# One tile instead of two for seven token sums, and the end of the output projection in a written order

## The chip, the core and the metric

The kernel runs on one core of a Trainium2 chip. The metric is the device time of one execution in microseconds (us), and the number compared is the median of the runs. A profiled execution leaves a trace with the start and duration of every instruction on the engines: TensorE (PE, and PEld for its weight loads), VectorE (DVE), ScalarE (ACT), GpSimd (POOL) and SyncE (SP, which issues the transfers).

## What is computed

Two residual blocks run over 256 latent tokens and 256 context tokens with 1024 features each. A block is a feed-forward network (FFN), a mixer, and a second FFN; the mixer is a short convolution in block 0 and grouped attention in block 1. In block 1 the context ends after the attention's keys and values. Ahead of each of the three parts stands the same normalization, and it is what the change is about:

```python
def _rms(t, g):
    t32 = t.astype(jnp.float32)
    y = t32 * lax.rsqrt(jnp.mean(t32 * t32, axis=-1, keepdims=True) + NORM_EPS)
    return y.astype(t.dtype) * g

def _modulate(t, g, shift, scale):
    return _rms(t, g) * (1 + scale) + shift

def _swiglu(h, w13, w2):
    gte, up = jnp.split(h @ w13, 2, axis=-1)
    return (jax.nn.silu(gte) * up) @ w2
```

So for every token the squares of its 1024 features are summed (a token sum), and the features are divided by the root of their mean.

## The kernel before, in words

The activations `x` lie transposed: 128 features on the partitions, eight row tiles (`KT`, counted by k or m), and 512 columns, the two streams s = 0 (latents) and s = 1 (context) of 256 tokens each. Matrix products are kept near float32 by splitting each operand into a rounded high part and a low part and adding three products (`mm3`, L146 to L148). ScalarE makes the high parts (L122 `wh<-wr` for weights) and VectorE the low parts (L123 and L526 `wl<-wr,wh`, L496 `bl<-hr,mod,bh` for activations).

**How a token sum is made.** While a projection writes new row tiles of `x`, ScalarE squares each tile and VectorE adds the squares into one tile `acc`. Seven of the eight squares are added this way; the last stays in a tile of its own. The sum over the 128 partitions is then made on TensorE: `sums_of` (L264) multiplies each 128-token piece, as stationary operand, with a column of ones, and for each of the two pieces it accumulates over two tiles, `acc` and the last square. That is four matmuls for one stream, and a float32 matmul leaves two records in the trace. ScalarE takes the root (L272 `rs<-ss`), VectorE the reciprocal (L279 `ri<-rs`), and `rms_rows` (L284 `ss<-cst,ri`) spreads it over the partitions on TensorE again.

**Borders.** Four of the five later norms lie in a border: `open_border` writes, for both streams, the last two row tiles of the old part's projection and the beginning of the next part in one order by hand, which holds for TensorE, VectorE, ScalarE and SyncE. There `late` is the matmuls of a row tile, `fin` (L452) adds the gated result into `x`, `square` (L460) squares it, `add` (L465) adds the first of the two squares into `acc`, `sums`, `root`, `inv` and `rows` make the norm, `mult` (L481) applies it, and `hi` (L488) and `lo` (L496) make the parts that the next matmuls read; `whi` and `wlo` (L521, L526) split the next weights; `share` puts in units of other work for VectorE (L165). The border after a projection with 8 tiles (the convolution's) is `short`, the others have 11. The borders are (block, part): (0,1), (0,2), (1,0) and (1,1). The four calls of `sums(0)` and the four of `sums(1)` are eight token sums. `sums(1)` stands in the next part, behind 16 matmuls that need stream 0 alone (L545), and behind it come 8 that read the first four low parts of stream 0.

**The ninth sum** is that of the last FFN (1,2). Its norm is taken out of the matmuls: the FFN's first products (`first_mm`) read the scaled `x` (`xa`) before the norm is known, and the root is applied to the products. It follows the attention's output projection, whose loop over m the scheduler orders; then a block in written order begins. The token sum stands between the fourth and the fifth row tile of the first FFN product.

**The start.** The very first norm has its own code (L1159), for which `fill` (L1080) puts 17 matmuls on a constant tile ahead of everything, with the spreading of a vector (L1272) behind them.

## Time and profile before

| what | value |
|---|---|
| median of 3 runs | 1550.32 us (1549.9 to 1550.5) |
| the profiled execution | 1550.0 us, span 1548.2 us |
| granted TensorE clock | 1.000 |
| busy: PE, PEld, DVE, ACT, POOL | 1543.1, 1417.7, 1309.1, 763.4, 28.9 us |
| records of the nine later token sums (L264) | 72 of 10286 |

The span is the time from the program's first instruction to its last; the execution's own time is 1.8 us longer. In a row of the timeline stand start, duration, engine, line, operation, output and inputs, shapes and a count, and in brackets the idle time of that engine ahead of it with what ended it. Records of one engine overlap a little, so that the next start can lie ahead of an end.

### The profile page before, as it was taken

The numbers are of one execution on the slowest core, as the hardware profiler recorded it, in microseconds if no ns is written. First come the engines' busy times: TensorE is split into PE (matmuls) and PEld (weight loads), VectorE is DVE, ScalarE is ACT, GpSimd is POOL, SyncE is SP. The second block draws the span as 40 slices with busy tenths as digits, with TensorE's granted clock in tenths as the row PEclk, the third lists the DMA queues.
The fourth block names the chain that finished last, engine by engine and source line by source line (L and its number), as shares of the span: only waits on it lengthen the run. The fifth ranks groups of instructions, "written<-read, shape, count | busy, mean of one in ns | idle before, by whom it ended". The sixth has DMA issues, their size and how long they took to land.

```text
span 1548.2 us, 25395 instructions
## 1 busy us (share of the span) xinstructions
PE 1543.1 (100%) x10286; PEld 1417.7 (92%) x10286; DVE 1309.1 (85%) x1946; ACT 763.4 (49%) x1286; POOL 28.9 (2%) x24
## 2 busy tenths in 40 slices
PE   9999999999999999999999999999999999999999
PEld 7899899989888899988999899988999899998888
DVE  6988889987999689987998989987998777888653
ACT  5554255536222475532554475522554365776551
POOL 0000000000000000000000000000000002220000
PEclk9999999999999999999999999999999999999999
DMA  9333633354565323355333633356444743256551
GB/s 358 136 112 131 209 124 121 125 195 171 183 215 201 136 92 114 114 183 193 123 128 125 224 111 109 115 185 232 137 134 172 260 153 120 97 185 244 189 175 71
DMA packets 52005, 247.72 MB, mean 160 GB/s; under 512 B 6064, under 2 KB 9264, under 8 KB 36656
## 3 DMA queue, kind: packets, MB, share of 16 engines
q1 hardware_dynamic: 51600, 245.91, 46.3%
q8 instruction: 80, 1.31, 0.4%
q14 instruction: 37, 0.30, 0.1%
q10 hardware_dynamic: 288, 0.19, 0.0%
HBM read 243.72 MB, written 1.05 MB: 158 GB/s over the span
## 4 chain that ended last, share of the span: by engine, by line
PE 99%; DMA 0%; ACT 0%; DVE 0%; issue 0%; DVEq 0%; ACTq 0%
PE py L146 9%; PE py L147 9%; PE py L148 9%; PE p L146 7%; PE p L148 7%; PE p L147 7%; PE q L148 5%; PE q L146 5%; PE q L147 5%; PE py L1997 3%; PE pu L1997 3%; PE pg L1997 3%; PE pg L1318 1%; PE pv L146 1%; PE pv L148 1%; PE pg L545 1%
## 5 line engine op out<-in xcount | busy, mean ns | idle before, releaser
L165 DVE CUSTOM_DVE_ANT_0 junk<-wm,scbc,cst 128x1024 bf16<-128x1024 f32 x224 | 286.8, 1281 | 32.1 <-DMA wm<-in_modT 30.5
L122 ACT ACTIVATE wh<-wr 128x1024 fp32r<-128x1024 f32 (+1 forms) x196 | 177.6, 925 | 213.5 <-PE py L147 130.4
L123 DVE TENSOR_TENSOR wl<-wr,wh 128x1024 fp32r<-128x1024 f32 (+1 forms) x196 | 205.4, 1059 | 52.2 <-PE py L1997 22.9
L146 PE MATMUL py<-gh,wh 128*128 128x512 f32 (+1 forms) x594 | 217.8, 367 | 0.0
L147 PE MATMUL py<-gl,wh 128*128 128x512 f32 (+1 forms) x594 | 217.3, 366 | 0.0
L148 PE MATMUL py<-gh,wl 128*128 128x512 f32 (+1 forms) x594 | 217.1, 365 | 0.0
L773 ACT ACTIVATE wh<-wr 128x1024 fp32r<-128x1024 f32 x165 | 169.5, 1056 | 85.6 <-DVE wr L796 67.4
L776 DVE TENSOR_TENSOR wl<-wr,wh 128x1024 fp32r<-128x1024 f32 x165 | 196.7, 1217 | 15.3 <-ACT wh L773 15.3
L148 PEld LDWEIGHTS py<-gh,wl 128*128 128x128 f32 x594 | 112.0, 189 | 18.0
L146 PEld LDWEIGHTS py<-gh,wh 128*128 128x128 f32 x594 | 112.1, 189 | 17.7
L147 PEld LDWEIGHTS py<-gl,wh 128*128 128x128 f32 x594 | 112.1, 189 | 17.2
L148 PE MATMUL p<-th,wl 128*128 128x256 f32 x440 | 124.5, 283 | 0.0
L147 PE MATMUL p<-tl,wh 128*128 128x256 f32 x440 | 124.5, 283 | 0.0
L146 PE MATMUL p<-th,wh 128*128 128x256 f32 x440 | 124.5, 283 | 0.0
L146 PE MATMUL q<-bh,wh 128*128 128x256 f32 x304 | 86.0, 283 | 0.0
L147 PE MATMUL q<-bl,wh 128*128 128x256 f32 x304 | 86.0, 283 | 0.0
L148 PE MATMUL q<-bh,wl 128*128 128x256 f32 x304 | 86.0, 283 | 0.0
L146 PEld LDWEIGHTS p<-th,wh 128*128 128x128 f32 x440 | 84.5, 192 | 0.2
L147 PEld LDWEIGHTS p<-tl,wh 128*128 128x128 f32 x440 | 84.5, 192 | 0.2
L148 PEld LDWEIGHTS p<-th,wl 128*128 128x128 f32 x440 | 84.5, 192 | 0.0
L791 DVE TENSOR_TENSOR wr<-wr 128x1024 f32<-128x1024 f32 x55 | 67.4, 1225 | 1.7
L148 PE MATMUL q<-th,wl 128*128 128x256 f32 x220 | 62.9, 286 | 0.0
(394 smaller groups left out, 4095.6 us busy)
## 6 DMA issues: line engine op xcount, KB each, us to landing
wr<-in_w SPq DMA_DIRECT2D x85, 1024.0 KB, 4.8
wm<-in_modT SPq DMA_DIRECT2D x128, 512.0 KB, 4.2
wr<-in_w2h SPq DMA_DIRECT2D x48, 704.0 KB, 4.2
wr<-in_cw_cx SPq DMA_DIRECT2D x8, 1024.0 KB, 4.9
wr<-in_w2l SPq DMA_DIRECT2D x8, 1024.0 KB, 5.0
mr<-in_mod SPq DMA_DIRECT2D x8, 512.0 KB, 9.1
wr<-in_cw_b SPq DMA_DIRECT2D x4, 1024.0 KB, 5.2
wr<-in_cw_out SPq DMA_DIRECT2D x4, 1024.0 KB, 5.6
```

Source lines behind the costliest of these rows:

```text
L122: nc.scalar.activation(out=hi, in_=src, func=AF.Copy)
L123: nc.vector.tensor_tensor(out=lo, in0=src, in1=hi.bitcast(F32), op=ALU.subtract)
L146: nc.tensor.matmul(ps, wh, mh, start=first, stop=False, **kw)
L147: nc.tensor.matmul(ps, wh, ml, start=False, stop=False, **kw)
L148: nc.tensor.matmul(ps, wl, mh, start=False, stop=last, **kw)
L165: nc.vector.tensor_tensor_reduce(out=junk, in0=raw, in1=scbc[:, v, :], scale=0.5 if ch in HALVED else 1.0, scalar=modb[:, l, col : col + 1 ...
L545: nc.tensor.matmul(ps, w[n == 1], hl if n == 2 else hh, start=first and n == 0 and k == ks[0] and (first is True or g == 0), stop=last and ...
L773: nc.scalar.activation(out=self.shaped(g, 0), in_=self.part(g), func=AF.Copy)
L776: nc.vector.tensor_tensor(out=self.shaped(g, 1), in0=self.part(g), in1=self.shaped(g, 0).bitcast(F32), op=ALU.subtract,)
L791: tt(out=by_two(raw[:, :1024]), in0=a21.unsqueeze(1).to_broadcast([P, 2, T2]), in1=by_two(raw)[:, :, :T2], op=ALU.subtract,)
L1318: nc.tensor.matmul(pps[i][j][:, c0:c1], w_at(i, (1 - j) * 1024 + k * P)[n == 1], hl if n == 2 else hh, start=k == n == c0 == 0, stop=k == ...
L1997: nc.tensor.matmul(p[:, :n], w(j, k)[part], m(k)[:, :n], start=not part and k == 0, stop=part == 1 and k == nk - 1, skip_group_check=True,)
```

## The change

Seven of the nine later token sums are made from `acc` alone. In the borders the second square is now added into `acc` by VectorE as well (`merge`), right behind its `square`; for stream 0 in all four borders, for stream 1 in (0,2) and (1,0) only (`joint`). There the add stands between the first two and the next two low parts. `sums_of` gets a list of one tile instead of two, and so has two matmuls instead of four. In the short border `square(1, 0)` and its add now stand ahead of the shared unit of VectorE's.

In the last norm the eighth square is added into `acc` too. To place it, the last two row tiles of the output projection move out of the scheduled loop into the written order: both tiles' matmuls, then per tile the gated add, the square and the high part, then per tile the add, the low part and the small shift columns. Two `fill` matmuls are put ahead of the first norm's sums.

```diff
     def square_add(k, c0, c1):
+        add_last(square_of(k, c0, c1), c0, c1)
...
         nc.scalar.activation(out=sq[:, :n], in_=x[:, k, c0:c1], func=AF.Square)
-        if k < KT - 1:
-            acc = accs["t"][:, c0:c1]
-            nc.vector.tensor_tensor(out=acc, in0=acc, in1=sq[:, :n], op=ALU.add)
-        else:
-            accs[c0 // S, "last"] = sq[:, :n]
+        return sq
...
-            self.quiet = (l, j) == (1, 1)
+            self.quiet, self.joint = (l, j) == (1, 1), j != 1
...
+        def merge(self, s):
+            self.add(s, 1)
+            del self.sq[1, s]
+
         def sums(self, s):
-            self.ss[s] = sums_of((accs[s], self.sq[1, s]))
+            self.ss[s] = sums_of([accs[s]] + [self.sq[i, s] for i in (1,) if (i, s) in self.sq])
...
         bd.fin(1, 0)
+        bd.square(1, 0)
+        bd.merge(0)
         if short:
             share(1)
-        bd.square(1, 0)
         bd.late(1, 0, range(mid))
...
-        bd.lo(low, 0)
+        bd.lo((0, 1), 0)
+        if bd.joint:
+            bd.merge(1)
+        bd.lo((2, 3), 0)
...
         spread_c(0, 13)
+        fill(idle, 2)
...
-    for m in range(KT):
-        if m == KT - 2:
-            ready()
-        if m < 2:
-            ps = py2[:, m, :]
-        else:
-            w = wo(m)
-            ps = psum("py")
-            for k in range(KT):
-                mm3(ps[:, :S], w(k), aos[k], k == 0, k == KT - 1)
+    for m in range(KT - 2):
+        ps = py2[:, m, :] if m < 2 else out_mm(m)
...
+    wo(KT - 2)
     ws13 = {0: load_w(a["w13"][1, 1, 0])}
     with tc.manual_schedule(engines=set(QUEUES[:3])):
+        ends = [out_mm(m) for m in (KT - 2, KT - 1)]
+        ready()
+        sqs = []
+        for m in (KT - 2, KT - 1):
+            gated(m, ends.pop(0)[:, :S], gate)
+            sqs.append(square_of(m, 0, S))
+            xa_hi(m)
+        for m in (KT - 2, KT - 1):
+            add_last(sqs.pop(0), 0, S)
+            xa_lo(m)
+            xa_shift(m)
         for i in range(FIRST):
...
-                half_way = sums_of((accs[0], accs[0, "last"]))
+                half_way = sums_of((accs[0],))
```

Three places show how this moves the instructions; nothing moves on the queues of SP and POOL. The first is VectorE's queue in border (1,0), from the gated add of stream 0's second tile to the low parts; `sq` is a square, `hr` the scaled activations, `bl` the low parts and `wl` those of weights. Before:

```order
L452 SCALAR_TENSOR_TENSOR x<-py_9023,mod_8_5018,x 128x256
L279 RECIPROCAL ri_9108<-rs_9091 128x2
L526 TENSOR_TENSOR wl_9084<-wr_8969,wh_9083 128x1024
L452 SCALAR_TENSOR_TENSOR x<-py_9064,mod_8_5018,x 128x256
L481 TENSOR_TENSOR hr_8890<-hr_8890,ss_9086 128x1024
L526 TENSOR_TENSOR wl_9114<-wr_8969,wh_9113 128x1024
L465 TENSOR_TENSOR acc_8675<-acc_8675,sq_9152 128x256
L481 TENSOR_TENSOR hr_8891<-hr_8891,ss_9086 128x1024
L452 SCALAR_TENSOR_TENSOR x<-py_9117,mod_8_5018,x 128x256
L496 SCALAR_TENSOR_TENSOR bl_9156<-hr_8890,mod_0_5759,bh_9155 128x256 x2
L496 SCALAR_TENSOR_TENSOR bl_9160<-hr_8890,mod_0_5759,bh_9159 128x256 x2
```

With the change, from the new add of stream 0 to the same low parts:

```order
L469 TENSOR_TENSOR acc_8674<-acc_8674,sq_9060 128x256
L283 RECIPROCAL ri_9106<-rs_9089 128x2
L534 TENSOR_TENSOR wl_9084<-wr_8968,wh_9083 128x1024
L456 SCALAR_TENSOR_TENSOR x<-py_9064,mod_8_5019,x 128x256
L489 TENSOR_TENSOR hr_8889<-hr_8889,ss_9086 128x1024
L534 TENSOR_TENSOR wl_9112<-wr_8968,wh_9111 128x1024
L469 TENSOR_TENSOR acc_8674<-acc_8674,sq_9150 128x256
L489 TENSOR_TENSOR hr_8890<-hr_8890,ss_9086 128x1024
L456 SCALAR_TENSOR_TENSOR x<-py_9115,mod_8_5019,x 128x256
L504 SCALAR_TENSOR_TENSOR bl_9154<-hr_8889,mod_0_5758,bh_9153 128x256 x2
L469 TENSOR_TENSOR acc_8674<-acc_8674,sq_9169 128x256
L504 SCALAR_TENSOR_TENSOR bl_9158<-hr_8889,mod_0_5758,bh_9157 128x256 x2
```

One add stands ahead of the reciprocal, and another between the low parts 0, 1 and 2, 3; all else keeps its place. The second place is TensorE's queue in the same border, where the sum of stream 1 stands between the next part's products. Before:

```order
L545 MATMUL pu_9189<-bh_9155,wl_9084 128x256 x2
L545 MATMUL pu_9189<-bh_9159,wl_9084 128x256 x2
L264 MATMUL ss_9211<-ones,acc_8675 128x1
L264 MATMUL ss_9211<-ones,sq_9171 128x1
L264 MATMUL ss_9211<-ones,acc_8675 128x1
L264 MATMUL ss_9211<-ones,sq_9171 128x1
L545 MATMUL pg_9188<-bl_9156,wh_9113 128x256 x2
```

With the change:

```order
L553 MATMUL pu_9188<-bh_9153,wl_9084 128x256 x2
L553 MATMUL pu_9188<-bh_9157,wl_9084 128x256 x2
L268 MATMUL ss_9210<-ones,acc_8674 128x1 x2
L553 MATMUL pg_9187<-bl_9154,wh_9111 128x256 x2
L553 MATMUL pg_9187<-bl_9158,wh_9111 128x256 x2
```

Two of the four matmuls are gone, and the first now reads an `acc` that was added to just before. The third place is the last norm. ScalarE's queue before, from the square of row tile 6 to the root (`wh` is the high part of the second FFN weight tile):

```order
L252 ACTIVATE sq_14183<-x 128x256
L2043 ACTIVATE xa_13972<-x,A_13974 128x256
L2049 CAST xa_13973<-bs 128x2
L122 ACTIVATE wh_14240<-wr_14238 128x1024
L122 ACTIVATE wh_14242<-wr_14238 128x1024
L252 ACTIVATE sq_14216<-x 128x256
L2043 ACTIVATE xa_13972<-x,A_13974 128x256
L272 ACTIVATE rs_14277<-ss_14272,eps_t 128x2
```

With the change:

```order
L260 ACTIVATE sq_14217<-x 128x256
L2050 ACTIVATE xa_13968<-x,A_13970 128x256
L260 ACTIVATE sq_14221<-x 128x256
L2050 ACTIVATE xa_13968<-x,A_13970 128x256
L2063 CAST xa_13968<-bs 128x2 x3
L2063 CAST xa_13969<-bs 128x2
L122 ACTIVATE wh_14237<-wr_14235 128x1024
L122 ACTIVATE wh_14239<-wr_14235 128x1024
L276 ACTIVATE rs_14272<-ss_14269,eps_t 128x2
```

Both squares stand ahead of the two weight splits, and the root right behind the splits. VectorE's queue there, before, from the gated add of row tile 6:

```order
L2010 SCALAR_TENSOR_TENSOR x<-py_14157,mod_5_10735,x 128x256
L255 TENSOR_TENSOR acc_13980<-acc_13980,sq_14183 128x256
L2044 SCALAR_TENSOR_TENSOR xa_13972<-x,A_13974,xa_13972 128x256
L2010 SCALAR_TENSOR_TENSOR x<-py_14190,mod_5_10735,x 128x256
L123 TENSOR_TENSOR wl_14241<-wr_14238,wh_14240 128x1024
L123 TENSOR_TENSOR wl_14243<-wr_14238,wh_14242 128x1024
L2044 SCALAR_TENSOR_TENSOR xa_13973<-x,A_13974,xa_13972 128x256
L279 RECIPROCAL ri_14279<-rs_14277 128x2
```

With the change:

```order
L2023 SCALAR_TENSOR_TENSOR x<-py_14164,mod_5_10732,x 128x256
L2023 SCALAR_TENSOR_TENSOR x<-py_14189,mod_5_10732,x 128x256
L248 TENSOR_TENSOR acc_13976<-acc_13976,sq_14217 128x256
L2056 SCALAR_TENSOR_TENSOR xa_13968<-x,A_13970,xa_13968 128x256
L248 TENSOR_TENSOR acc_13976<-acc_13976,sq_14221 128x256
L2056 SCALAR_TENSOR_TENSOR xa_13969<-x,A_13970,xa_13968 128x256
L123 TENSOR_TENSOR wl_14238<-wr_14235,wh_14237 128x1024
L123 TENSOR_TENSOR wl_14240<-wr_14235,wh_14239 128x1024
L283 RECIPROCAL ri_14274<-rs_14272 128x2
```

The two weight splits, which stood ahead of the last `xa`, now stand behind it and right ahead of the reciprocal.

More of the change, by code (lines that the diff above doesn't have):

```diff
@@ L242, in square_add, with add_last, square_of @@
     def square_add(k, c0, c1):
+        add_last(square_of(k, c0, c1), c0, c1)
+    def add_last(sq, c0, c1):
+        if sq is not None:
+            acc = accs["t"][:, c0:c1]
+            nc.vector.tensor_tensor(out=acc, in0=acc, in1=sq[:, : c1 - c0], op=ALU.add)
+    def square_of(k, c0, c1):
         n = c1 - c0
@@ L461, in square, with add @@
             self.scaled(6 + i, s)
-        def add(self, s):
+        def add(self, s, i=0):
             acc = accs[s]
-            nc.vector.tensor_tensor(out=acc, in0=acc, in1=self.sq[0, s], op=ALU.add)
+            nc.vector.tensor_tensor(out=acc, in0=acc, in1=self.sq[i, s], op=ALU.add)
+        def merge(self, s):
+            self.add(s, 1)
+            del self.sq[1, s]
         def sums(self, s):
-            self.ss[s] = sums_of((accs[s], self.sq[1, s]))
+            self.ss[s] = sums_of([accs[s]] + [self.sq[i, s] for i in (1,) if (i, s) in self.sq])
         def root(self, s):
@@ L2027, in hybrid_kernel, with out_mm, xa_hi, xa_lo @@
     split(bs[:, 0, :], bs[:, 1, :], B[:, :, 0])
-    for m in range(KT):
-        if m == KT - 2:
-            ready()
-        if m < 2:
-            ps = py2[:, m, :]
-        else:
-            w = wo(m)
-            ps = psum("py")
-            for k in range(KT):
-                mm3(ps[:, :S], w(k), aos[k], k == 0, k == KT - 1)
+    def out_mm(m):
+        w = wo(m)
+        ps = psum("py")
+        for k in range(KT):
+            mm3(ps[:, :S], w(k), aos[k], k == 0, k == KT - 1)
+        return ps
+    def xa_hi(m):
+        nc.scalar.activation(
+            out=xa(m, 0)[:, :S], in_=x[:, m, :S], func=AF.Identity, scale=A[:, m, :1]
+        )
+    def xa_lo(m):
+        hi, lo = xa(m, 0), xa(m, 1)
+        nc.vector.scalar_tensor_tensor(
+            out=lo[:, :S], in0=x[:, m, :S], scalar=A[:, m, :1], in1=hi[:, :S].bitcast(F32),
+            op0=ALU.mult, op1=ALU.subtract,
+        )
+    def xa_shift(m):
+        for part in range(2):
+            nc.scalar.copy(
+                xa(m, part)[:, S:], bs[:, part, m : m + 1].bitcast(F32).to_broadcast([P, 2])
+            )
+    for m in range(KT - 2):
+        ps = py2[:, m, :] if m < 2 else out_mm(m)
         gated(m, ps[:, :S], gate)
@@ L2041, in hybrid_kernel @@
         square_add(m, 0, S)
-        hi, lo = xa(m, 0), xa(m, 1)
-        nc.scalar.activation(out=hi[:, :S], in_=x[:, m, :S], func=AF.Identity, scale=A[:, m, :1])
-        nc.vector.scalar_tensor_tensor(
-            out=lo[:, :S], in0=x[:, m, :S], scalar=A[:, m, :1], in1=hi[:, :S].bitcast(F32),
-            op0=ALU.mult, op1=ALU.subtract,
-        )
-        for part, t in enumerate((hi, lo)):
-            nc.scalar.copy(
-                t[:, S:], bs[:, part, m : m + 1].bitcast(F32).to_broadcast([P, 2])
-            )
+        xa_hi(m)
+        xa_lo(m)
+        xa_shift(m)
     gts = []
@@ L2129, in shifted_lo @@
         )
+    wo(KT - 2)
     ws13 = {0: load_w(a["w13"][1, 1, 0])}
     with tc.manual_schedule(engines=set(QUEUES[:3])):
+        ends = [out_mm(m) for m in (KT - 2, KT - 1)]
[4 more added lines that the diff above has]
+            sqs.append(square_of(m, 0, S))
+            xa_hi(m)
+        for m in (KT - 2, KT - 1):
+            add_last(sqs.pop(0), 0, S)
+            xa_lo(m)
+            xa_shift(m)
         for i in range(FIRST):
```

## The prediction

> **What bounds the kernel now.** I read the page first, then its chain of waits, then the token sums by tile, and last the timeline around each of the seven places.

> ```profile
> span 1548.2 us, 25395 instructions
> PE 1543.1 (100%) x10286; PEld 1417.7 (92%) x10286; DVE 1309.1 (85%) x1946; ACT 763.4 (49%) x1286; POOL 28.9 (2%) x24
> ```

> Of the chain of waits:

> ```profile
> PE 99%; DMA 0%; ACT 0%; DVE 0%; issue 0%; DVEq 0%; ACTq 0%
> ```

> TensorE is busy for 1543.1 of 1548.2 us, and 99% of the chain that ended last is its own. So a TensorE instruction taken away shortens the run by what it takes there, as long as the others deliver in time; work given to VectorE costs nothing where VectorE waits anyway. The question is the price of a sum, and whether any engine is late at the seven places.

> **The matmuls removed.** The tile view lists the token sums, and the timeline the end of the first one. A count of x2 in a row is one float32 matmul with its two records.

> ```profile
> L264 PE MATMUL ss<-ones,acc x36: 168/250/250, 367.6 to 1362.3; 128*128 128x1 f32 x36
> L264 PE MATMUL ss<-ones,sq x36: 250/250/250, 367.7 to 1362.5; 128*128 128x1 f32 x36
> ```

> ```profile
> 367.97 0.36 PE L264 MATMUL ss<-ones,acc 128*128 128x1 f32 x2
> 368.19 0.36 PE L264 MATMUL ss<-ones,sq 128*128 128x1 f32 x2
> 368.42 0.36 PE L146 MATMUL py<-gh,wh 128*128 128x256 f32 x1
> ```

> 36 records are 18 matmuls over `acc` and 18 over the last square, two of each in a sum. Their ends overlap, so I take starts: from 367.97 to 368.42 there are two matmuls, 0.225 us each (0.224 with the starts unrounded). Seven sums lose two: 14 x 0.224 = 3.14 us, 0.45 a sum. That is 0.203% of the run, and 0.2% (3.10 us) is about what a measurement of this kernel can tell from no change.

> [...]

> **The adds.** Seven more adds of 128x256 on VectorE (six in the borders, one at the end) take this long each:

> ```profile
> L465 DVE TENSOR_TENSOR acc<-acc,sq x8: 418/422/426, 364.1 to 1250.4; 128x256 f32<-128x256 f32 x8
> ```

> They are 2.95 us of VectorE work. An add begins 0.035 us after the square ends, and the first weight load of the sum can begin about 0.05 us after the add; so a sum is possible 0.42 + 0.09 = 0.51 us after the square. Border (0,1), stream 0:

> ```profile
> 366.17 0.42 ACT L460 ACTIVATE sq<-x 128x256 f32<-128x256 f32 x1 [1.67 <-DVE x L452]
> 367.49 0.19 PEld L264 LDWEIGHTS ss<-ones,acc 128*128 128x128 f32 x1
> 368.97 0.17 DVE L279 RECIPROCAL ri<-rs 128x2 f32<-128x2 f32 x1 [2.84 <-ACT rs L272]
> ```

> The square ends at 366.59, the sum can start at 367.10, TensorE comes at 367.49: 0.39 spare, in VectorE's idle stretch of 2.84 us. (1,0) and (1,1) have the same shape. Three sums keep all of their 0.45. The short border (0,2):

> ```profile
> 546.73 0.49 DVE L452 SCALAR_TENSOR_TENSOR x<-py,mod,x 128x256 f32<-128x256 f32 x1 [0.46 <-PE py L148]
> 547.14 1.27 DVE L165 CUSTOM_DVE_ANT_0 junk<-wm,scbc,cst 128x1024 bf16<-128x1024 f32 x1
> 547.25 0.42 ACT L460 ACTIVATE sq<-x 128x256 f32<-128x256 f32 x1 [1.03 <-DVE x L452]
> 548.21 0.31 PEld L264 LDWEIGHTS ss<-ones,acc 128*128 128x128 f32 x2
> 549.61 0.17 DVE L279 RECIPROCAL ri<-rs 128x2 f32<-128x2 f32 x1 [1.20 <-ACT rs L272]
> ```

> The square ends at 547.67, the sum can start at 548.18, TensorE comes at 548.21: just covered. The unit of 1.27 us waits behind the add now and ends at about 549.4 instead of 548.42. The reciprocal behind it then starts at about 549.3, still ahead of 549.61, and TensorE spreads it later than that. Cost 0.

> Stream 1 is tighter, because its add stands in a full VectorE queue. In (0,2):

> ```profile
> 554.22 2.06 DVE L496 SCALAR_TENSOR_TENSOR bl<-hr,mod,bh 128x256 fp32r<-128x256 f32 x5
> 554.61 0.40 ACT L460 ACTIVATE sq<-x 128x256 f32<-128x256 f32 x1
> 555.49 0.19 PEld L264 LDWEIGHTS ss<-ones,acc 128*128 128x128 f32 x1
> ```

> All this comes 0.45 earlier, since stream 0's sum is shorter and this chain follows TensorE there. The square then ends at 554.56, the sum can start at 555.07, TensorE comes at 555.04: 0.03 lost. The low parts 2 and 3 are 0.4 later, but TensorE reads them behind the sum, at 555.8 and 555.9, and they end at 555.4 and 555.8.

> In (1,0) the chain cannot follow:

> ```profile
> 895.90 1.06 ACT L521 ACTIVATE wh<-wr 128x1024 fp32r<-128x1024 f32 x1 [0.75 <-ACT hr L435]
> 896.86 0.24 ACT L272 ACTIVATE rs<-ss,eps_t 128x2 f32<-128x2 f32 x1
> 897.22 1.22 DVE L526 TENSOR_TENSOR wl<-wr,wh 128x1024 fp32r<-128x1024 f32 x1
> 898.65 0.48 DVE L452 SCALAR_TENSOR_TENSOR x<-py,mod,x 128x256 f32<-128x256 f32 x1 [0.21 <-PE py L148]
> 901.71 1.22 DVE L481 TENSOR_TENSOR hr<-hr,ss 128x1024 f32<-128x1024 f32 x1
> 903.02 0.91 ACT L488 ACTIVATE bh<-hr,mod 128x256 fp32r<-128x256 f32 x2 [0.95 <-DVE hr L481]
> 903.83 0.40 ACT L460 ACTIVATE sq<-x 128x256 f32<-128x256 f32 x1
> 904.65 0.19 PEld L264 LDWEIGHTS ss<-ones,acc 128*128 128x128 f32 x1
> ```

> The root of stream 0 stands behind a weight split that starts when TensorE is done with the products ahead of the sum, which doesn't move. Root, reciprocal and low parts hold VectorE until 898.45, so the gated add at 898.65 comes only its 0.2 of idle time plus 0.08 of overlap earlier, 0.28. The scaling at 901.71, the high parts and the square follow by as much: the square ends at 903.95, the sum can start at 904.46, TensorE comes at 904.20. It waits 0.26 of the 0.45.

> **The last norm.** ScalarE and VectorE go through the two weight splits, ahead of root and reciprocal:

> ```profile
> 1358.88 0.50 ACT L2043 ACTIVATE xa<-x,A 128x256 fp32r<-128x256 f32 x1
> 1359.36 2.00 ACT L122 ACTIVATE wh<-wr 128x1024 fp32r<-128x1024 f32 x2
> 1362.77 0.26 ACT L272 ACTIVATE rs<-ss,eps_t 128x2 f32<-128x2 f32 x1 [0.70 <-PE ss L264]
> ```

> VectorE there:

> ```profile
> 1360.45 2.36 DVE L123 TENSOR_TENSOR wl<-wr,wh 128x1024 fp32r<-128x1024 f32 x2
> 1363.12 0.15 DVE L279 RECIPROCAL ri<-rs 128x2 f32<-128x2 f32 x1
> ```

> And TensorE's weight load that reads the reciprocal:

> ```profile
> 1364.72 0.19 PEld L284 LDWEIGHTS ss<-cst,ri 128*128 128x128 f32 x1
> ```

> The last square and high part (0.8 us) and three more small copies (0.25) now stand ahead of the splits, with a wait for row tile 7. The high parts then begin at about 1360.75 instead of 1359.36, the low parts at 1361.85 instead of 1360.45, and they hold VectorE until 1364.2. The reciprocal, a full us later than now, ends at about 1364.27; its weight load can begin at 1364.32. TensorE comes at 1364.72 - 0.45 = 1364.27. So 0.05 is lost (0 to 0.3, by whether the splits begin 0.1 earlier or 0.25 later). The sum itself is safe: both adds are done by 1360.8. The transfer that waits for the split tile's buffer goes out 1.4 us later; its tile is used two products on.

> **The fills.**

> ```profile
> 9.68 0.28 PE L1272 MATMUL cs<-cst,sccol 128*128 128x128 f32 x1
> 10.46 1.95 PE L1159 MATMUL ss<-ones,sq 128*128 128x1 f32 x16 [0.51 <-DVE sq L1155]
> ```

> TensorE waits for VectorE's squares here. Two fills are four records of 0.11, from 9.79 to 10.24: inside the wait. Cost 0; at worst 0.1, if each took twice that as the very first do, and no gain, since the first sums run at 0.11 a record already.

> **Sum.** 3.14 - 0.03 - 0.26 - 0.05 = 2.80 us. The profiled execution's own 1550.0 (span 1548.2 and 1.8 around it) becomes 1547.2. It lies 0.3 under the median, so I give the median 1550.32 - 2.80 = 1547.5.

> **Rivals.** First, all is hidden: the stalls of 0.34 come out as nothing, the gain is 3.1 or more, 1547.2 or less. For it: each stall is a few steps of 0.1 long. Against it: the wait in (1,0) comes from a queue that I can follow step by step.

> Second, VectorE keeps TensorE back in the two joint borders. By the stretches they are full, and behind the sums VectorE still waits for TensorE by only this:

> ```profile
> 548.00:575.00 27.00, 27.00 (x218) 26.51 (x217) 23.55 (x38) 22.30 (x47) 0.00 (x0) 1.00 0.17 59
> 895.00:923.00 28.00, 28.00 (x231) 27.74 (x231) 24.51 (x37) 23.19 (x48) 0.00 (x0) 1.00 0.29 96
> ```

> ```profile
> 560.01 1.22 DVE L481 TENSOR_TENSOR hr<-hr,ss 128x1024 f32<-128x1024 f32 x1 [0.21 <-PE ss L284]
> ```

> VectorE is busy for 23.55 of 27 and 24.51 of 28 us. If both borders give back their 0.9, the gain is 3.14 - 1.79 - 0.05 = 1.3: 1549.0. Against it: behind 560.01 the high parts that TensorE needs next are 1.8 us early.

> Third, on the other side: the adds are exposed. If a square comes so late that TensorE waits for the whole add, each place loses 0.51 and gains 0.45; seven make +0.4 us, 1550.7. It decides once the mean wait passes 0.45. The 0.39 spare in three borders speaks against it.

> Fourth, only the narrow products are saved, because their weight loads would hide under the wide matmuls around. The cheapest records of the run then give the price:

> ```profile
> 12.34 1.08 PE L1171 MATMUL pr<-mr,sccol 128*32 128x128 f32 x32
> ```

> 1.08 us for 32 is 0.034 each; 28 of them are 0.95, less the stalls of 0.34 a gain of 0.6: 1549.7. Against it stand the 0.112 measured between the very records that go. [...]

> **How the numbers follow.** Forecast (1547.2 to 1548.2) 0.57, all hidden 0.20, VectorE 0.16, exposed adds 0.04 (of which 0.02 by more than 0.2%), narrow products 0.03. Faster by over 0.2% is the second case, 0.20; slower by over 0.2% is 0.02; the rest, 0.78, lies within. The range runs from full saving with no stall and 0.3 beyond (1546.9) to VectorE's case (1549.1).

> **What would show it.** 44 records of the sums instead of 72 (36 over `acc`, 8 over a square), 112 ns apart. In (1,0) a TensorE wait of about 0.26 on the add at stream 1's sum, and almost none in (0,2) and at the other five. The last reciprocal near 1364.3 less the lead of some 2.4 us gained by then, right ahead of its matmul. TensorE's idle time at the first sums cut from 0.51 to under 0.2. I am wrong if a new wait of over 0.3 stands at any sum, or if the lead shrinks in a border's second half.

## The result, and the profile after

| | before | after |
|---|---|---|
| median of 22 runs each, same chip | 1550.21 us | 1548.16 us |
| lowest and highest run | 1549.90 and 1551.02 | 1547.10 and 1549.56 |
| profiled execution, its span | 1550.0, 1548.2 | 1548.16, 1546.3 |
| records of the nine later sums | 72 | 44 |

The ratio is 0.9986, with a 95% interval of 0.9979 to 0.9992: 2.05 us faster, 0.13%, which is less than the 0.2% taken as the bound of what can be told from no change. The forecast was 1547.5 and a range of 1546.9 to 1549.1. The new runs spread over 2.5 us, the old ones over 1.1; that spread turned out to be the more interesting half of this case.

The view of the sums' line in the kernel after (operation, tiles, count, duration in ns):

```profile
L268 PE MATMUL ss<-ones,acc x36: 168/250/271, 367.9 to 1360.1; 128*128 128x1 f32 x36
L268 PE MATMUL ss<-ones,sq x8: 250/250/250, 376.6 to 1252.6; 128*128 128x1 f32 x8
```

36 records over `acc` are left as before, and only 8 of the 36 over a square. To see what each sum gave, the table compares the start of its first matmul in both traces. The lead is after minus before.

| sum | before, us | after, us | lead | what the step behind it gave |
|---|---|---|---|---|
| (0,1) stream 0 | 367.61 | 367.91 | +0.30 | 0.45 |
| (0,1) stream 1 (two tiles still) | 376.61 | 376.46 | -0.15 | -0.05 |
| (0,2) stream 0 | 548.33 | 548.23 | -0.10 | 0.45 |
| (0,2) stream 1 | 555.61 | 555.06 | -0.55 | 0.46 |
| (1,0) stream 0 | 895.77 | 894.76 | -1.01 | 0.10 |
| (1,0) stream 1 | 904.77 | 903.66 | -1.11 | 0.35 |
| (1,1) stream 0 | 1244.82 | 1243.36 | -1.46 | 0.45 |
| (1,1) stream 1 (two tiles still) | 1253.82 | 1251.91 | -1.91 | 0 |
| last norm | 1361.79 | 1359.88 | -1.91 | 0.36 |
| last FFN, second part | 1388.84 | 1386.57 | -2.27 | |

The steps add up to 2.57 us. But the lead starts at +0.30, so the new kernel was late before its first changed sum, and at the last matmul it is only 1.87 us (1544.63 against 1542.76): 0.40 is given back behind 1389 us. So there are three things to explain: the 2.57, the late start, and the loss at the end.

**The start.** TensorE's timeline after, up to the first sums (start, duration, count):

```profile
1.07 6.70 PE L1092 MATMUL idle<-sones 128*128 128x128 f32 x34 [1.07 <-DVE eps_t L105]
7.60 3.07 PE L1284 MATMUL cs<-cst,sccol 128*128 128x128 f32 x26
10.50 0.61 PE L1092 MATMUL idle<-sones 128*128 128x128 f32 x4
10.95 1.84 PE L1171 MATMUL ss<-ones,sq 128*128 128x1 f32 x16
```

And of the kernel before:

```profile
1.06 5.75 PE L1080 MATMUL idle<-sones 128*128 128x128 f32 x34 [1.06 <-DVE eps_t L105]
```

The same 34 records take 6.70 us instead of 5.75. In both traces they begin 213 ns apart and end 112 ns apart; the step changes at 4.63 us in the one run and at 6.61 us in the other. At these same moments the trace's first record of the granted clock begins, with 1.0, and none stands ahead of it; this is what a rise of the clock means below. Nothing in the change touches this. TensorE arrives at the fills 0.71 us later, the wait that had hidden them is gone, and the sums start at 10.95 instead of 10.46.

**The end.** ScalarE and TensorE of the kernel after, in the last output projection:

```profile
1484.11 1.06 ACT L122 ACTIVATE wh<-wr 128x1024 fp32r<-128x1024 f32 x1 [0.77 <-DMA wr<-in_w2l]
1487.28 0.50 PE L2010 MATMUL py<-g,wh 128*128 128x512 f32 x1 [0.23 <-DVE g L123]
```

A weight tile lands late; the split that waits for it stands on ScalarE ahead of the last split of the FFN's product `g`, and TensorE waits for `g`. Before, the same wait on the tile was 0.36 and TensorE did not stop there.

### The profile page after: what moved, and what is told of

It reads as the page before. It is cut to its first block, busy times and chain, and to the rows that moved or that the text cites. A ratio compares the mean times of both kernels' runs of the same rounds, so it can differ in the third digit from the quotient of the medians.

```text
span 1546.3 us, 25363 instructions
## 1 busy us (share of the span) xinstructions
PE 1541.3 (100%) x10262; PEld 1416.0 (92%) x10262; DVE 1311.1 (85%) x1953; ACT 763.2 (49%) x1286; POOL 28.9 (2%) x24
## 4 chain that ended last, share of the span: by engine, by line
PE 98%; DVE 1%; ACT 0%; DMA 0%; issue 0%; DVEq 0%; ACTq 0%; SPq 0%
PE py L146 9%; PE py L147 9%; PE py L148 9%; PE p L146 7%; PE p L148 7%; PE p L147 7%; PE q L148 5%; PE q L146 5%; PE q L147 5%; PE py L2010 3%; PE pg L2010 3%; PE pu L2010 3%; PE pg L1330 1%; PE pv L146 1%; PE pv L148 1%; PE pv L147 1%
## 5 line engine op out<-in xcount | busy, mean ns | idle before, releaser
L165 DVE CUSTOM_DVE_ANT_0 junk<-wm,scbc,cst 128x1024 bf16<-128x1024 f32 x224 | 286.6, 1280 | 29.4 <-DMA wm<-in_modT 27.7
L122 ACT ACTIVATE wh<-wr 128x1024 fp32r<-128x1024 f32 (+1 forms) x196 | 177.5, 925 | 215.6 <-PE py L147 131.4
L123 DVE TENSOR_TENSOR wl<-wr,wh 128x1024 fp32r<-128x1024 f32 (+1 forms) x196 | 205.4, 1058 | 52.5 <-PE py L2010 22.7
L146 PE MATMUL py<-gh,wh 128*128 128x512 f32 (+1 forms) x594 | 217.8, 367 | 0.0
L148 PE MATMUL py<-gh,wl 128*128 128x512 f32 (+1 forms) x594 | 217.1, 365 | 0.0
L148 PEld LDWEIGHTS py<-gh,wl 128*128 128x128 f32 x594 | 112.0, 189 | 18.0
L146 PEld LDWEIGHTS py<-gh,wh 128*128 128x128 f32 x594 | 112.1, 189 | 17.5
L148 PE MATMUL p<-th,wl 128*128 128x256 f32 x440 | 124.5, 283 | 0.0
L146 PE MATMUL p<-th,wh 128*128 128x256 f32 x440 | 124.5, 283 | 0.0
L146 PE MATMUL q<-bh,wh 128*128 128x256 f32 x304 | 86.0, 283 | 0.0
L148 PE MATMUL q<-bh,wl 128*128 128x256 f32 x304 | 86.0, 283 | 0.0
L146 PEld LDWEIGHTS p<-th,wh 128*128 128x128 f32 x440 | 84.5, 192 | 0.2
L148 PEld LDWEIGHTS p<-th,wl 128*128 128x128 f32 x440 | 84.5, 192 | 0.0
L148 PE MATMUL q<-th,wl 128*128 128x256 f32 x220 | 62.9, 286 | 0.0
```

Source lines behind the costliest of these rows:

```text
L122: nc.scalar.activation(out=hi, in_=src, func=AF.Copy)
L123: nc.vector.tensor_tensor(out=lo, in0=src, in1=hi.bitcast(F32), op=ALU.subtract)
L146: nc.tensor.matmul(ps, wh, mh, start=first, stop=False, **kw)
L148: nc.tensor.matmul(ps, wl, mh, start=False, stop=last, **kw)
L165: nc.vector.tensor_tensor_reduce(out=junk, in0=raw, in1=scbc[:, v, :], scale=0.5 if ch in HALVED else 1.0, scalar=modb[:, l, col : col + 1 ...
```

## The experiments

Medians of about ten runs are uncertain by about 1.4 us here, so the verdicts rest on leads inside the profiles, and, for the start, on the granted clock that each run reports.

### The parts one at a time

Without the fills:

```diff
         spread_c(0, 13)
-        fill(idle, 2)
```

> The changed kernel without the two fills. Theory (clock and fills): TensorE's first matmuls step 213 ns, from some moment 112 ns; that moment was 4.64 us in the profile of before and about 6.6 us after, and the first sums came 0.49 us later (10.95 against 10.46). The two fills (4 records x 112 ns = 0.45 us) used up the 0.51 us of wait that had hidden a late moment. Without them the first sum starts at 10.46 to 10.50 whenever the clock rises: median 0.2 to 0.45 us below the changed kernel's 1548.16, about 1547.8, and a spread of runs nearer before's 1.1 us than 2.5 us. Rival (fills are free, the late start of the profile is chance): the same median, 1548.2, and the same spread. For the stall of 0.39 us at 1487 us (last FFN output projection): theory (landing of one weight transfer varies): it may be there or not; rival (it comes with the reordered last norm): it is there, 0.3 to 0.5 us.

The kernel before with the fills alone:

```diff
         spread_c(0, 13)
+        fill(idle, 2)
```

> The kernel before with the two fills alone. Theory (clock and fills): 0 when the clock rises as early as in the profile of before, 0.45 us when it rises late: median 1550.4 to 1550.6 and a spread wider than before's 1.1 us. Rival (fills are free): 1550.2. Stall in the last FFN output projection: theory (landing varies) may be there, by the rival (last norm's order) it is not.

Only the six merged sums of the borders, without the fills and with the last norm in the scheduler's order:

```diff
+        bd.square(1, 0)
+        bd.merge(0)
...
+        if bd.joint:
+            bd.merge(1)
```

> The kernel before with only the six merged sums in the joint borders, no fills and the last norm as it was. From the two profiles the lead grew to 1.91 us at the last of these sums with a start 0.31 us late, so 2.2 us are expected: 1548.0. By the prediction's terms (four times 0.45 less nothing at three, 0.45 at the stream 0 of (0,2), 0.42 and 0.19 at the two stream 1) 2.40 less: 1547.8. Rival (VectorE keeps TensorE back in the borders): 1549.0 or more.

And only the last norm (order by hand and merged sum):

```diff
+        ends = [out_mm(m) for m in (KT - 2, KT - 1)]
...
-                half_way = sums_of((accs[0], accs[0, "last"]))
+                half_way = sums_of((accs[0],))
```

> The kernel before with only the last norm changed: output tiles 6 and 7 ordered by hand and one sum from one tile. By the profiles the lead grew 0.44 us there (1.91 to 2.35): 1549.8; by the prediction's 0.40: 1549.8. Rival (the order set by hand costs the 0.39 us at 1487 us): 1550.2 and a stall of 0.3 to 0.5 us in the last FFN output projection, which the kernel before does not have.

| kernel | median of 11 runs | from the first `pr` products (12.34 us before) to the last FFN's second part |
|---|---|---|
| before | 1550.49 (33 runs) | 1376.50 |
| after (22 runs of its own) | 1548.16 | 1373.85 |
| without the fills | 1547.97 | 1373.87 |
| fills alone | 1550.62 | 1376.76 |
| borders alone | 1549.13 | (see below) |
| last norm alone | 1549.83 | 1376.09 |

Without the fills the median is 0.19 below the changed kernel's, at the edge of the 0.2 to 0.45 expected; with the fills alone it is 0.13 above the kernel before beside it, just over the 1550.4 to 1550.6 expected. Neither difference is clear of the uncertainty of such medians.

The right column leaves out the start and the end. By it the change is worth 2.63 to 2.65 us with and without fills, and the last norm alone 0.41; 0.04 to 0.08 of each lies ahead of the first changed sum, where nothing was changed, so that 2.57 to 2.59 and 0.36 are left for the sums. (The fills alone are 0.26 longer there; all of it went in the last norm, which took 27.34 us from the sum to the second part instead of 27.06, because TensorE waited between the two tiles for the last square in this one profile; the edit gives no reason for it.) The stall of the last projection was there without the fills (1.44 us) and in the borders alone (1.42), 0.25 us in the last norm alone, and none with the fills alone. So the rival that tied it to the reordered last norm falls: the kernel that has the reorder alone has little of it, and one without the reorder has 1.42.

The borders alone missed their 1548.0. Its profile shows why. First TensorE at the first sums, then its stretches (length, busy us and records of PE, PEld, DVE, ACT, POOL, then the granted clock):

```profile
10.34 2.15 PE L1175 MATMUL ss<-ones,sq 128*128 128x1 f32 x16 [0.40 <-DVE sq L1171]
```

```profile
10.00:11.00 1.00, 0.66 (x6) 0.66 (x6) 0.96 (x3) 1.00 (x3) 0.00 (x0) 1.00 0.97 379
11.00:12.00 1.00, 1.00 (x11) 1.00 (x10) 0.00 (x0) 0.65 (x2) 0.00 (x0) 0.97 1.00 330
12.00:13.00 1.00, 1.00 (x15) 0.95 (x18) 0.17 (x2) 0.26 (x1) 0.00 (x0) 0.50 1.04 418
14.00:15.00 1.00, 1.00 (x11) 0.71 (x4) 0.00 (x0) 0.58 (x2) 0.00 (x0) 0.50 1.04 374
15.00:16.00 1.00, 1.00 (x10) 1.00 (x8) 0.47 (x2) 0.41 (x2) 0.00 (x0) 0.83 1.14 404
```

The clock was halved at 11.93 us and came back at 15.34, 3.41 us later; it had risen at 5.10, 6.83 (twice 3.41) before the fall. The sum at 367.61 in the kernel before stands at 368.88 here, 1.27 us late, although no changed sum lies ahead of it. From there to the last norm's sum it takes 991.95 us, before 994.18: the six sums did give the 2.2 expected, 2.23, and the halved clock and the stall at the end took more than that back from this profile.

So 6.83 and 3.41 us stand between the changes of the clock in this trace. In the traces of before and after the record of the clock at 1.0 lasts 1542.824 and 1539.411 us, which is 452 and 451 times 3.4133. The fall came 1.59 us behind the end of a wait of 0.40 us, with one-column matmuls in between.

All traces together say more. Counted in steps of 3.41 us from the rise of the clock (the windows of the table, and all those below, are the author's estimate from these distances), TensorE's time in the window that holds most of the first sums reads:

| kernel | window, us | TensorE waits, us | one-column matmuls, us | clock behind it |
|---|---|---|---|---|
| borders alone | 8.52 to 11.93 | 0.40 | 1.59 | 0.5 |
| merge without the order (below) | 9.21 to 12.62 | 0.20 | 1.95 | 0.5 |
| order without the merge (below) | 9.44 to 12.85 | 0 | 1.95 | 1.0 |
| without the fills | 9.59 to 13.00 | 0 | 1.84 | 1.0 |
| before | 8.04 to 11.45 | 0.51 | 0.99 | 1.0 |

Every run also reports its mean granted clock, which lets all runs be sorted by it:

| kernels | runs | runs with a clock under 1.0 | their times |
|---|---|---|---|
| before | 53 | 9 | 1551.27 to 1551.57 (four at 0.999), 1552.71 to 1553.22 (five at 0.998) |
| without the fills, borders alone, last norm alone | 33 | 8 | 0.6 to 2.3 us above the median of the others of their kernel |
| with 17 at the start and two or four fills (after, fills alone, and below: the same again, four fills, stream 1, all nine) | 37 | 0 | |

The other runs of before lie at a median of 1550.21 to 1550.37 in their comparisons, so a window at half clock cost about 1.1 us in these runs and a second one some 1.4 more (3.41 us at half clock lower the mean over 1548 us by 0.001, so 0.999 is counted as one window and 0.998 as two). (1550.01 in the one run of the second comparison is counted among the 53. The 22 runs of before in the first table report no clock and are not. Of the two single runs below without fills, order and merge, the merge had it; they are not counted either.) With the fills the halving was not seen: none of 37 runs against 17 of 86, and the prediction had no term for it. But most of these runs were not made beside each other. On one chip and side by side stand 15 of 66 runs without fills and none of 11 with the fills alone, which chance alone gives in about one case of 13; and the 22 runs of before that ran beside the changed kernel's 22 all stayed below the 1551.27 of the fastest halved run, so the halving was rare there without fills too. That the fills keep the clock up is therefore likely, and the table of windows gives a reason for it, but it is not shown. Sorted so, the fills' price shows as well: the ten runs at full clock without them have a median of 1547.95, the 22 of the kernel after 1548.16. These two were not run beside each other, so the 0.2 is an indication.

### The same kernel again, and four fills

> The changed kernel once more, unaltered, for a second profile. Theory (the clock's rise varies from run to run, the fetch of instructions does not): the moment at which TensorE's step falls from 213 to 112 ns is another than 6.61 us, and the first sums start between 10.3 and 11.3 us, 0.47 us later for each us that the clock rises later than 5.3 us. A 16 KB instruction packet on one of the 16 DMA engines was issued 0.07 us ahead of the weight transfer at 1478.85 us, and its last part landed 5.17 us after issue (the other fifteen by 4.84); in the kernel without the fills it was 0.79 us behind the issue and the last part landed at 6.22. By the theory the packet is again within 0.2 us of the issue, and TensorE's stall in the last output projection 0.3 to 1.4 us. Rival (landing is chance): packet and stall anywhere.

```diff
-        fill(idle, 2)
+        fill(idle, 4)
```

> The changed kernel with four fills ahead of the first sums instead of two. Theory: the first sums start 0.45 us later than with two fills for the same rise of the clock: at 10.69 for an early rise (up to 5.3 us), 11.4 for one at 6.6 us; the granted clock stays 1.0 to the end. The four records are eight more instructions of TensorE, so the 16 KB instruction packet comes 0.9 us or more ahead of the weight transfer's issue in the last output projection: the stall there is under 0.3 us. Rival (fills are free): first sums at 10.3 to 10.5. Rival (landing is chance): the stall anywhere from 0 to 1.4 us.

The two runs took 1547.24 and 1548.15 us. From the first sum of (0,1) to the last FFN's second part the kernel run again gained 2.49 us over before, where the first profile has 2.57. The moment at which the step of TensorE's records changes, and the start of the first sums, over all profiles but two that come below:

| fills ahead of the sums | clock rises, us | first sums start, us |
|---|---|---|
| none | 4.63, 5.10, 5.79, 6.03, 6.18, 6.91 | 10.46, 10.34, 10.47, 10.24, 10.29, 10.64 |
| two | 4.34, 5.17, 5.37, 6.16, 6.61 | 10.31, 10.42, 10.35, 10.73, 10.95 |
| four | 6.32 | 11.25 |

Up to a rise at 5.4 us two fills cost nothing, because VectorE's squares set the start at 10.2 to 10.5. Later than that they cost up to 0.45: 10.73 against 10.29 for a rise at 6.16 and 6.18. Four fills cost another 0.45: by the two-fill line a rise at 6.32 gives 10.81 + 0.45 = 11.26, and 11.25 was measured. Between 6.16 and 6.61 the start moves by 0.22, 0.49 us for each us of a later rise, as expected from records of 213 and 112 ns. The rival "fills are free" falls.

In the same kernel run again, the rise at 4.34 gave this, where the kernel after had 10.50 and 10.95:

```profile
9.63 0.61 PE L1092 MATMUL idle<-sones 128*128 128x128 f32 x4
10.31 1.95 PE L1171 MATMUL ss<-ones,sq 128*128 128x1 f32 x16
```

For the end, the DMA records hold a packet of 16 KB of the kind "instruction". The table gives its start against the issue of the weight transfer that TensorE ends up waiting for, the landing of that transfer after its issue, and the time that TensorE's steps lose at that matmul.

| kernel | packet, us | landing, us | lost at that matmul, us |
|---|---|---|---|
| fills alone | -4.82 | 4.69 | 0 |
| last norm alone | -1.59 | 5.03 | 0.25 |
| before | -1.26 | 4.77 | 0 |
| four fills | -0.84 | 4.84 | 0.06 |
| after, again | -0.12 | 4.71 | 0 |
| after | -0.07 | 5.17 | 0.39 |
| borders alone | +0.04 | 6.19 | 1.42 |
| without the fills | +0.79 | 6.22 | 1.44 |

In the view of the weight loads, the time to landing (min, median, max) in the stretch of that transfer, after and again:

```profile
DMA to landing us min/median/max: 5.2/5.2/5.2
```

```profile
DMA to landing us min/median/max: 4.7/4.7/4.7
```

In the kernel without the fills, where the maximum belongs to that transfer, with the ScalarE split and the matmul behind it:

```profile
DMA to landing us min/median/max: 4.8/5.5/6.2
```

```profile
1484.52 1.06 ACT L122 ACTIVATE wh<-wr 128x1024 fp32r<-128x1024 f32 x1 [1.81 <-DMA wr<-in_w2l]
1487.70 0.50 PE L2009 MATMUL py<-g,wh 128*128 128x512 f32 x1 [1.27 <-DVE g L123]
```

Of that transfer's 16 parts fifteen landed by 4.70 us and one at 6.22; in the borders alone fifteen by 4.75 and one at 6.19. In the other six profiles it started 0.2 to 1.8 us ahead of the issue or 4.2 to 4.3 behind it, and 0 to 0.27 was lost. In this place the large losses, 1.42 and 1.44 us, came only where the packet started within the transfer's first 0.8 us (+0.04 and +0.79). Its place goes with the program: in the same kernel it came at -0.07 and -0.12, and with four fills (eight instructions more) 0.7 to 0.8 us earlier, where 0.9 was expected. But whether it hurts varies at nearly the same place (0.39, and 0 where the same kernel was expected to lose 0.3 to 1.4); and in the fills alone, at the transfer before this one, a packet at +0.74 came with a landing at 5.11.

All 1 MB weight transfers of the 14 traces (from 40 us on) tell how much of this is chance. Of 1099 of them with no such packet between 1 us ahead of the issue and 6 us behind it, 23 had their last part land 1 us or more behind the fifteenth. Of 98 with a packet within the first 1 us it was 28, and of 45 with one from 1 to 3.5 us it was 29. So here a packet that started during a transfer went with a late part far more often, and not only within the first 0.8 us; it was neither always followed by one nor the only thing that came with one. That the packet is the cause in each run is likely and not shown, since it could not be moved without moving other things.

The trace of before has 80 such packets of 16384 bytes, one per 128 pairs of weight load and matmul (the median between two of them). TensorE was busy for 1543.1 of its 1548.2 us, so the 80 together cost it 5.1 us of idle time at most; where one met a transfer that others wait for, up to 1.44 us were lost.

### Stream 1 of (1,0)

```diff
-            self.quiet, self.joint = (l, j) == (1, 1), j != 1
+            self.quiet, self.joint = (l, j) == (1, 1), (l, j) == (0, 2)
```

> The changed kernel with stream 1's sum of border (1,0) made from two tiles again. By the two traces the merge there gained 0.45 and lost 0.45 (a wait of 0.35 on the add, 0.10 more at the matmuls behind it), so the time from stream 0's sum of (1,0) to stream 0's sum of (1,1) stays within 0.05 of the changed kernel's 348.60 us. By the prediction's term (0.26 lost) it would be 0.19 us longer; if the wait were not caused by the add, 0.45 longer.

From stream 0's sum of (1,0) to that of (1,1) it took 348.58 us, after 348.60 and again 348.60. The merge there is worth nothing. In the kernel after, TensorE, VectorE and ScalarE read:

```profile
903.66 0.61 PE L268 MATMUL ss<-ones,acc 128*128 128x1 f32 x4 [0.19 <-DVE acc L469]
```

```profile
902.14 0.87 DVE L504 SCALAR_TENSOR_TENSOR bl<-hr,mod,bh 128x256 fp32r<-128x256 f32 x2
903.18 0.42 DVE L469 TENSOR_TENSOR acc<-acc,sq 128x256 f32<-128x256 f32 x1 [0.16 <-ACT sq L464]
```

```profile
901.93 0.91 ACT L496 ACTIVATE bh<-hr,mod 128x256 fp32r<-128x256 f32 x2 [0.95 <-DVE hr L489]
902.74 0.40 ACT L464 ACTIVATE sq<-x 128x256 f32<-128x256 f32 x1
```

The square ends at 903.14, the add at 903.60, the sum starts at 903.66. The step ahead of it is 0.35 us over the usual (the bracket's 0.19 is less because records of matmuls overlap). From there to the next border another 0.10 goes, and together they eat the 0.45. The run took 1547.11 us, the changed kernel beside it 1547.24.

### All nine sums merged

```diff
-            self.quiet, self.joint = (l, j) == (1, 1), j != 1
+            self.quiet, self.joint = (l, j) == (1, 1), True
```

> The changed kernel with all nine sums made from one tile: stream 1 of (0,1) and (1,1) too. There a modulation unit (1.28 us) and two low parts (0.84) stand on VectorE ahead of the add: it would end near 377.6 where TensorE comes at 376.46. Theory (VectorE's queue decides): TensorE waits 1.2 us at both, gains 0.45, so each border is 0.7 to 0.8 us longer and the lead at the last norm 1.5 us less. Rival (the low parts that follow wait anyway, 0.38 us of stall stands there already): 0.3 us each.

VectorE and TensorE in (0,1), stream 1:

```profile
376.18 0.88 DVE L504 SCALAR_TENSOR_TENSOR hl<-hr,mod,hh 128x256 fp32r<-128x256 f32 x2
376.98 0.41 DVE L469 TENSOR_TENSOR acc<-acc,sq 128x256 f32<-128x256 f32 x1
```

```profile
377.44 0.61 PE L268 MATMUL ss<-ones,acc 128*128 128x1 f32 x4 [0.99 <-DVE acc L469]
```

The step is 1.15 us over the usual, near the 1.2 expected. But from stream 0's sum of (0,1) to that of (0,2) only 0.32 us more passed than after (180.64 against 180.32), and from (1,1) stream 0 to the last norm 0.36 (116.88 against 116.52). That is the rival's 0.3: the stall of 0.38 that stood behind this sum, on the same low parts, disappears into the longer wait (1.15 - 0.45 - 0.38 = 0.32). The run took 1548.30 us. The two sums that the change left alone are rightly left.

### Order and merge in the last norm

The order by hand, with the sum still made from two tiles:

```diff
         for m in (KT - 2, KT - 1):
-            add_last(sqs.pop(0), 0, S)
+            if m < KT - 1:
+                add_last(sqs.pop(0), 0, S)
```

> The kernel before with output tiles 6 and 7 ordered by hand as in the changed kernel, but the last sum made from two tiles as before (no fills, no merged sums). Theory (the order itself is neutral, the gain is the merge): from the last sum's start to the first product of the last FFN's second part 27.05 us as before, within 0.1, where the merge alone made it 0.34 to 0.44 shorter. Rival (the order costs, since reciprocal and high parts come a us later): 0.3 to 1.0 us longer.

And the merge in the scheduler's order, in the kernel before:

```diff
-        if k < KT - 1:
-            acc = accs["t"][:, c0:c1]
-            nc.vector.tensor_tensor(out=acc, in0=acc, in1=sq[:, :n], op=ALU.add)
-        else:
-            accs[c0 // S, "last"] = sq[:, :n]
+        acc = accs["t"][:, c0:c1]
+        nc.vector.tensor_tensor(out=acc, in0=acc, in1=sq[:, :n], op=ALU.add)
```

> The kernel before with the last norm's sum made from one tile, but without the order by hand. The add of the last square then stands on VectorE behind two weight splits that end at 1362.8 us: it ends near 1363.2, TensorE comes to the sum at 1361.79. Theory (the queue ahead of the add decides): TensorE waits about 1.4 us there and saves 0.45, so the last norm is 0.9 to 1.1 us longer than before: near 1551.0. Rival (the order by hand was not needed): 0.4 us shorter.

With the order alone the run took 1550.03 us, and it is 27.06 us from the sum to the second part, before 27.05: the order costs nothing and brings nothing by itself. The merge without it took 1555.57 us. VectorE and TensorE there:

```profile
1363.35 2.36 DVE L123 TENSOR_TENSOR wl<-wr,wh 128x1024 fp32r<-128x1024 f32 x2
1365.63 0.42 DVE L254 TENSOR_TENSOR acc<-acc,sq 128x256 f32<-128x256 f32 x1
```

```profile
1366.19 0.58 PE L261 MATMUL ss<-ones,acc 128*128 128x1 f32 x4 [1.71 <-DVE acc L254]
```

The add stands behind the two weight splits, as expected, and from (1,1)'s stream 1 to this sum it is 109.84 us instead of 107.97: 1.87 lost. From the sum to the second part another 1.18 goes (28.23 against 27.05), though the sum itself is 0.45 shorter. The stretches show where:

```profile
1364.00:1366.00 2.00, 0.48 (x5) 0.28 (x3) 2.00 (x4) 0.97 (x3) 0.00 (x0) 1.00 0.16 66
1368.00:1371.00 3.00, 3.00 (x16) 3.00 (x15) 0.00 (x0) 0.13 (x1) 0.00 (x0) 0.50 0.58 246
```

TensorE waited for 1.71 us, and the clock was halved from 1367.71 to 1371.12. So this wait cost itself, and then came 3.41 us at half clock. (This run also had two such windows at the start, 12.62 to 19.45, 2.5 us by the lead at the first sum of (0,1); they are the rest of its 5.6 us.) The expected 0.9 to 1.1 lacked the clock, and its wait of 1.4 was too small by 0.4 to 0.5.

### Fewer fills at the start

```diff
-WARM = 17
+WARM = 12
...
-        fill(idle, 2)
```

> The changed kernel without the two fills and with 12 in place of 17 at the start: TensorE waits longer ahead of the first sums. Theory (a window of 3.41 us with too little matmul work in it halves the granted clock): TensorE waits 0.5 to 1.5 us there, most runs have a stretch of 3.4 us at a clock of 0.5 between 8 and 16 us, which the profile shows, and the first stages end 1.2 to 1.7 us later; median 1548.5 to 1549.6. Rival (a wait ahead of the first sums costs nothing, VectorE's squares set them anyway): first sums at 10.3 whatever the clock, granted clock 1.0 throughout, median 1547.2 to 1547.9.

And the same with seven fills ahead of the sums:

```diff
-WARM = 17
+WARM = 12
...
-        fill(idle, 2)
+        fill(idle, 7)
```

> As the kernel with 12 fills at the start, but with 7 ahead of the first sums, so that TensorE has as many as the changed kernel and hardly waits. Theory: granted clock 1.0 throughout, median 1547.6 to 1548.4, about the changed kernel's. Rival (the clock falls at random, whatever the fills): stretches at 0.5 as often as with 12 and none.

| | runs at clock 1.0 | runs at 0.998 or 0.999 |
|---|---|---|
| 12, none | 4: 1547.13 to 1547.55 | 6: 1549.57 to 1550.67 |
| 12, seven | 9: 1548.04 to 1549.85 | 1: 1551.99 |

With 12 and none the median of all ten is 1549.62, at the upper end of the 1548.5 to 1549.6 expected. The two groups do not overlap; their medians are 1547.42 and 1549.79, 2.4 us apart for two windows. That decides against the rival, by which the clock was to stay at 1.0 throughout. The theory's rule, that too little matmul work in a window halves the clock, fits the two groups and is not shown by them. With seven fills the clock held in nine of ten. But the median of 1549.51 is above what was expected of it, and the profiles (12 and none first, then 12 and seven) show that the pair is no clean control:

```profile
6.62 3.14 PE L1284 MATMUL cs<-cst,sccol 128*128 128x128 f32 x26 [1.02 <-ACT table L1097]
10.29 1.95 PE L1171 MATMUL ss<-ones,sq 128*128 128x1 f32 x16 [0.53 <-DVE sq L1167]
```

```profile
6.57 3.14 PE L1284 MATMUL cs<-cst,sccol 128*128 128x128 f32 x26 [0.98 <-ACT table L1097]
9.55 1.73 PE L1092 MATMUL idle<-sones 128*128 128x128 f32 x14
11.11 1.84 PE L1171 MATMUL ss<-ones,sq 128*128 128x1 f32 x16
```

After 12 fills TensorE also waits a us for ScalarE ahead of the spreading (L1284), so both kernels have a second wait in the windows so counted, and the seven fills start too late to fit: sums at 11.11 even with the clock up at 4.41. Which of the two waits goes with the halved clock of six runs of the first kernel stays open: its one profile is of a run at full clock. In both profiles the wait of 1.0 us ahead of L1284 lay whole in one window, with wide matmuls around it, and the clock stayed up. The reason for the second kernel's five runs between 1549.4 and 1549.9 at full clock stays open too; a later rise of the clock, as seen at up to 6.91 us in other kernels, would fit, but only one of its runs was profiled, with the rise at 4.41.

## Why the prediction was right, and where it was off

The forecast stood 0.66 us under the measured median, inside its range and with the right sign. The kernel before ran at 1550.21 beside it instead of 1550.32. That the range held the result is in part luck: its upper end was set by the case of VectorE keeping TensorE back, which did not occur, and of the two places that made most of the difference from the forecast, the start had a term of 0 and the end none at all. By its steps:

- **The price of a sum, 0.45 us: right.** Four sums gave 0.45 or 0.46 and the remaining records stand as forecast. The rival that took only the narrow product's price is out.
- **Full 0.45 in stream 0 of (0,1), (1,0), (1,1), and "just covered" in (0,2): right.** In the profile above 0.05 went between stream 1 of (0,1) and stream 0 of (0,2), and the same in its second profile; in six others with these sums nothing went there.
- **Stream 1 of (0,2), 0.03 lost: right** within 0.05 (it gave 0.46 of 0.45).
- **Stream 1 of (1,0), "it waits 0.26 of the 0.45": right place, too small.** The wait was 0.35, and 0.10 more was lost behind it, which the step did not look for. A new wait of over 0.3 at a sum was also the prediction's own sign of being wrong; at this one sum it is met. The chain is the one it followed (weight split, root, reciprocal, low parts, gated add), but it took the gated add to come 0.28 earlier beyond the lead of 1.01, and it came 0.02 earlier (897.62 against 898.65). The split ahead of the root started 0.32 us after its wait ended instead of 0.04, and the trace shows nothing that it waits for in that time, so why stays open. The sum made from two tiles there takes the same time (348.58 against 348.60). The term is mis-sized by 0.19. After, ScalarE's split and VectorE's gated add read:

```profile
895.16 1.06 ACT L529 ACTIVATE wh<-wr 128x1024 fp32r<-128x1024 f32 x1 [1.03 <-issue]
```

```profile
897.62 0.48 DVE L456 SCALAR_TENSOR_TENSOR x<-py,mod,x 128x256 f32<-128x256 f32 x1
```

- **The last norm, 0.05 lost: nearly right.** It gave 0.36, so 0.09 was lost. The chain came as worked out: weight splits on VectorE from 1359.98, the reciprocal, and its weight load on TensorE.

```profile
1359.98 2.36 DVE L123 TENSOR_TENSOR wl<-wr,wh 128x1024 fp32r<-128x1024 f32 x2 [0.81 <-ACT wh L122]
1362.26 0.15 DVE L283 RECIPROCAL ri<-rs 128x2 f32<-128x2 f32 x1
```

```profile
1362.47 0.52 PEld L288 LDWEIGHTS ss<-cst,ri 128*128 128x128 f32 x4
```

  The forecast end of the reciprocal less the 1.91 gained by then is 1362.36; it ended at 1362.41.
- **The fills, "Cost 0; at worst 0.1": wrong.** This is the step that failed. It took the 0.51 us of wait in the one profile for the cover that every run has. The cover was gone where TensorE's clock rose at 6.16 us instead of up to 5.4, and there the fills cost about 0.45 (10.73 against 10.29). The step also took the fills for worthless, and they probably keep the clock from being halved, which befell 9 of 53 runs of the kernel before.
- **The end was not in the sum at all.** The rows quoted ended with the last norm. With fewer matmuls a block of instructions came beside a weight transfer 100 us later, and 0 to 1.4 us were lost there in the profiles; that the one causes the other is likely and not shown.

The sum forecast was 2.80 and the sums gave 2.57. From 1550.21 that would be 1547.64; the other 0.52 of the median lies in the start (0 to 0.45) and the end (0 to 0.39 in the two profiles of this kernel), which also make the wider spread. Of the rivals, VectorE keeping TensorE back would have shown in the right column of the first experiments' table, and it does not. "All is hidden" fell with (1,0). Exposed adds would have shown as a wait of about 0.5 at each sum, and only the one in (1,0) has a wait.

No version clearly beat the changed kernel. Leaving out the merge at stream 1 of (1,0) gives the same time with less work for VectorE.

## What to carry to other kernels

A wait in a profile is cover for added work only if it is there in every run: ask what set both of its ends, and if one end is the clock's rise (4.34 to 6.91 us here), take several profiles. Waits of 0.20 and 0.40 us on TensorE next to matmuls of one column came with 6.83 and 3.41 us at half clock behind them here (one of 0.51 did not), so read the granted clock of every run, and price fillers by that too. When matmuls are taken away, look for late landings of transfers far behind the change, and judge each part by leads between fixed points of two traces. Here most steps repeated to 0.05 us from profile to profile, with one stray of 0.28, where medians of ten runs did not tell 1.

## What was not expected of the hardware

- The clock rose at 4.34 to 6.91 us in the profiles, 3.3 to 5.8 us after the first matmul, and each us later made the first sums about 0.49 us later with fills.
- It fell again inside a busy stretch: with a wait of 0.40 us ahead of 16 one-column records (from 11.93 for 3.41 us), with one of 0.20 us there (from 12.62 for 6.83 us), and with a wait of 1.71 us (from 1367.71 for 3.41 us). One window cost about 1.1 to 1.3 us at the start.
- One block of instructions (16 KB) beside a 1 MB weight transfer came with a landing at 6.2 us instead of 4.7, through one of its 16 parts. Over the 14 traces 28 of 98 transfers with a block in their first 1 us had such a part, against 23 of 1099 without a block near.
